# VectorE makes every low part of the weights, low parts of the input projection are re-read from DRAM, and the work is put in a new order

## The chip, the cores and the metric

The kernel runs on one core of a Trainium2 chip. The metric is the device time of one execution in microseconds; the median of three runs counts. Five engines work side by side: TensorE (PE in the rows; its weight loads are PEld), VectorE (DVE), ScalarE (ACT), GpSimd (POOL) and SyncE (SP), which here does nothing but issue DMAs. Each engine takes its instructions strictly in their order; an instruction that has to wait holds up all that stand behind it on its engine.

## The reference, cut to what matters

One layer of a decoder trunk over a prompt of 1040 tokens (16 learned ones ahead) and 32 sample tokens, all float32:

```python
def _layer(x, ...):
    xn = _rms(x, norm1_g)
    u = jnp.einsum('bld,de->ble', xn, w_in)              # input projection, 1024 -> 2816
    u_tm, u_lx, u_lg = jnp.split(u, [D_TM_PROJ, D_TM_PROJ + D_LRU], axis=-1)
    y_tm, ... = _rwkv7(u_tm, ...)                        # matrix recurrence over the tokens, 8 heads of 64
    y_lru, ... = _rglru(u_lx, u_lg, ...)                 # gated linear recurrence over the tokens
    x = x + jnp.einsum('ble,ed->bld', jnp.concatenate([y_tm, y_lru], axis=-1), w_out)
    xn = _rms(x, norm2_g)
    up = jnp.einsum('bld,df->blf', xn, ffn_w_up)         # 1024 -> 3072
    upc, ... = _causal_dwconv(up, ffn_conv, ffn_conv_w, ffn_conv_b)
    hid = jax.nn.gelu(upc) * jnp.einsum('bld,df->blf', xn, ffn_w_gate)
    x = x + jnp.einsum('blf,fd->bld', hid, ffn_w_down)
    return x, ...
```

Outputs are the normed activations and five kinds of state.

## The kernel before, in words

**Matmuls and low parts.** Each weight is split into a high part `wh` (rounded to the fast matmul format) and a low part `wl`, the rest; activations are split likewise. `load_w` (L529 to L540) brings 1024 x 128 weights in two halves of 256 KB: a DMA into `wraw` (L534), a ScalarE copy that rounds into `wh` (L537), and a subtraction that makes `wl` (L538), on VectorE for the first half and on GpSimd for the second. `wraw`, `wh` and `wl` have rings of four halves, that is two calls. `mm_tile` (L542) adds three products for each of eight slices of 128 rows, `wl` by the activation's high part (L546), `wh` by the same (L547), `wh` by its low part (L548), into one PSUM bank `mmb`; there are two such banks.

**The first stage** (everything up to the line with `issue_in_order`) is written as steps in the list `ORDER`. Tokens come in two pieces, of 560 and of 512. `x` norms and transposes a piece (`xt`, `xh`, `xl`, L517 to L524); `p`, `q` and `l` are its input projection, 22 calls of `load_w` for each piece, so that each weight of `w_in` is loaded, rounded and split twice; `proj` computes a tile in the piece's two column chunks `chk` (280 and 280, or 256 and 256) and a ScalarE copy empties each bank into `stage` (L755). `u` is a unit of the matrix recurrence (four heads, up to 256 tokens): a long run of VectorE work, small matmuls, and two round trips through DRAM (`zd` to `Dq`, `xd` to `WD`). `r` is the gated recurrence. `w` is the output projection for a quarter of the tokens (L1410 to L1423), `n` and `f` (`fac`, L1467 to L1476) an early part of the up and gate projections, and `e` the last quarter of `w_out` with the second norm (`xn`, `n2h`, `n2l`, L1547 to L1551).

**What sets the order.** `plan` takes the steps' instructions and what each must wait for, gives each instruction a duration from `cost`, and schedules them engine by engine, those with the longest way to the end first; what it finds is fixed as each engine's order. It holds GpSimd and VectorE apart where both read SBUF through operands. For a GpSimd subtraction that writes the fast matmul format, `cost` gives VectorE's duration.

**The second stage** (`up_gate`, `down`) is written out: up and gate projection of 128 columns at a time, the rest of the tokens, then the down projection (L1642 to L1645).

Of the kernel before, what the change touches and what calls it, by code (L numbers as in the profile page):

```python
# [12 lines left out]
F32 = mybir.dt.float32  # L13
F32R = mybir.dt.float32r
# [7 lines left out]
P = 128  # L22
# [28 lines left out]
class Piece:  # L51
    def __init__(self, idx, g0, gw):
        self.idx, self.g0, self.gw = idx, g0, gw
        self.chk = [(0, gw // 2), (gw // 2, gw // 2)]
# [23 lines left out]
ORDER = [('l', 0), ('p', 0, 0), ('u', 0, 0, 0), ('u', 0, 0, 1), ('q', 0, 0, 1), ('r', 0, 0), ('u', 0, 0, 2), ('p', 0, 1), ('r', 0, 1), ('q', 0, 2, 3), ('x', 1), ('r', 0, 2), ('l', 1), ('u', 0, 1, 0), ('q', 1, 0, 1), ('p', 1, 1), ('u', 0, 1, 1), ('r', 0, 3), ('u', 0, 1, 2), ('r', 1, 0), ('u', 1, 1, 0), ('p', 1, 0), ('q', 1, 2, 3), ('w', 0), ('n',), ('u', 1, 1, 1), ('f', 0, 0), ('f', 0, 1), ('u', 1, 0, 0), ('f', 1, 0), ('f', 2, 0), ('f', 1, 1), ('r', 1, 1), ('f', 3, 0), ('f', 2, 1), ('w', 1), ('f', 3, 1), ('f', 4, 0), ('f', 5, 0), ('u', 1, 0, 1), ('r', 1, 2), ('f', 4, 1), ('f', 5, 1), ('f', 6, 0), ('r', 1, 3), ('w', 2), ('f', 7, 0), ('e',), ('f', 6, 1), ('f', 7, 1)]  # L78
# [9 lines left out]
STREAM, FILL = 1.05, 10.8  # L88

TOGETHER = {}  # L90
TABLES = {"Exp": "e", "Sqrt": "s", "Gelu_apprx_tanh": "g"}
# [100 lines left out]
def cost(x):  # L192
# [7 lines left out]
    if e == "PE":  # L200
# [5 lines left out]
        side = 1  # L206
        if i[0].dtype == F32R:
            parts, cols, w = 1, n * STREAM + FILL, n
        elif getattr(x, "is_transpose", False):
            parts, cols, w = 1, 2 * n, 2 * n * (k == P)  # L210
        else:
            parts, cols, w = 2, 2 * n, 4 * n * (k >= 64)
            side = P // min(shape)
            cols += side * FILL * (side > 1)
# [4 lines left out]
    if e == "Activation":  # L219
        return (0.051 if psum else 0.093) + n / 1200 + 0.093 * s, None  # L220
    if e == "DVE" or o and o[0].dtype == F32R:
        fast = len(i) - s < 2 and not psum and "Memset" not in type(x).__name__
        return 0.069 + n / (1920 if fast else 960) + 0.061 * s, None
# [149 lines left out]
def hymba_kernel(ctx: ExitStack, tc: tile.TileContext, ins, outs, dbg=None):  # L373
# [156 lines left out]
    def load_w(src, c0):  # L530
        hs = []
        for k in (0, 4):
# [5 lines left out]
            (G if k else V).tensor_sub(l, raw, h.bitcast(F32))  # L538
# [20 lines left out]
    r = 0  # L559
# [190 lines left out]
    def proj(pc, xn, ti, func=AF.Copy):  # L750
        wh, wl = load_w(w_in, P * ti)
# [630 lines left out]
    def wout(pc, tmp, x1=None, stage=None):  # L1382
# [13 lines left out]
        for m in range(8):  # L1396
            wh, wl = load_w(w_out, P * m)
# [354 lines left out]
```

## Time and profile before

| | us |
|---|---|
| median of three runs (lowest to highest) | 1641.05 (1639.43 to 1644.85) |
| the profiled execution, its own time | 1638.3 |
| its span, first to last instruction | 1636.6 |
| TensorE busy in it | 1516.7 |
| VectorE busy | 1049.6 |
| ScalarE busy | 739.7 |
| GpSimd busy | 406.9 |

The span is read in stretches: the first piece's input projection up to about 230 us, a changeover to the second piece (230 to 300), the second piece's input projection (300 to 500), output projection and early up and gate projection (500 to 917), and the second stage from 917 to the end. For each stretch the table of windows gives what each engine was busy, the clock that TensorE was granted (1.00 is 2.4 GHz, 0.50 is 1.2 GHz; a stretch between shows a mixture of the two), and the load of the DMA engines. What TensorE was not busy in a stretch, and what its clock was below 1.00, is time that another order or other durations could give back.

### The profile page before, as it was taken

The page shows a single profiled execution, that of the slowest core. Times are in us where ns is not written, and L with a number is a line of the kernel's source. Part 1 is how long each engine was busy: PE and PEld are TensorE (multiplying, and loading weights), DVE is VectorE, ACT ScalarE, POOL GpSimd, SP SyncE. Part 2 cuts the span into 40 slices and gives each one's busy share as a digit, 9 for nine tenths or more (in the row PEclk, how much of TensorE's full clock was granted, in tenths as well). Part 3 has the DMA queues.
Part 4 walks back from the last instruction along what each step waited for, and adds up shares of the span by engine and source line. Part 5 has one row for each costly group of instructions (what it writes and reads, how often), then busy time and mean ns, then how long its engine had stood idle before and what let it go on. Part 6 is the DMA issues. An engine that isn't in the chain of part 4 may idle for free. (4 is left out here: it accounts for less than half of the span.)

```text
span 1636.6 us, 32363 instructions
## 1 busy us (share of the span) xinstructions
PE 1516.7 (93%) x12364; PEld 1428.5 (87%) x12364; DVE 1049.6 (64%) x2306; ACT 739.7 (45%) x1577; POOL 406.9 (25%) x580
## 2 busy tenths in 40 slices
PE   5999988999988978888897999999999999999997
PEld 5988876888877877777787899999999999999996
DVE  7376768877872999699568654554554455455446
ACT  4457377565653666567555433223223223222312
POOL 4232224332324433544344211011001001101101
PEclk9999989999999989999999999999999999999999
DMA  6544334444555445645577421121122112212102
GB/s 167 156 127 123 109 92 123 142 131 116 145 147 144 138 124 138 188 127 149 159 197 204 144 86 55 55 66 56 56 62 66 52 55 68 60 55 63 39 17 108
DMA packets 321791, 176.35 MB, mean 108 GB/s; under 512 B 70088, under 2 KB 309436, under 8 KB 321604
## 3 DMA queue, kind: packets, MB, share of 16 engines
q1 hardware_dynamic: 315796, 172.56, 37.0%
q10 hardware_dynamic: 5840, 1.73, 0.5%
q8 instruction: 97, 1.59, 0.4%
q14 instruction: 58, 0.48, 0.1%
HBM read 143.57 MB, written 30.85 MB: 107 GB/s over the span
## 5 line engine op out<-in xcount | busy, mean ns | idle before, releaser
L538 POOL TENSOR_TENSOR wl<-wraw,wh 128x512 fp32r<-128x512 f32 x172 | 230.0, 1338 | 343.2 <-ACT wh L537 330.1
L537 ACT ACTIVATE wh<-wraw 128x512 fp32r<-128x512 f32 x344 | 213.2, 627 | 166.5 <-PE mmb L548 112.2
L546 PE MATMUL mmb<-n2h,wl 128*128 128x400 f32 (+1 forms) x768 | 265.6, 346 | 3.8 <-DVE fac L1467 3.8
L548 PE MATMUL mmb<-n2l,wh 128*128 128x400 f32 (+1 forms) x768 | 265.9, 346 | 0.0
L547 PE MATMUL mmb<-n2h,wh 128*128 128x400 f32 (+1 forms) x768 | 265.3, 345 | 0.0
L538 DVE TENSOR_TENSOR wl<-wraw,wh 128x512 fp32r<-128x512 f32 x172 | 135.7, 789 | 168.4 <-ACT wh L537 166.1
L1645 DVE TENSOR_TENSOR x<-x,mmb 128x352 f32<-128x352 f32 (+3 forms) x288 | 149.5, 520 | 88.6 <-PE mmb L1644 82.9
L1642 PE MATMUL mmb<-hh,dl 128*128 128x352 f32 (+3 forms) x576 | 188.9, 328 | 1.7 <-DVE x L1645 0.4
L1643 PE MATMUL mmb<-hh,dh 128*128 128x352 f32 (+3 forms) x576 | 186.7, 324 | 0.0
L1644 PE MATMUL mmb<-hl,dh 128*128 128x352 f32 (+3 forms) x576 | 186.3, 323 | 0.0
L546 PE MATMUL mmb<-xh,wl 128*128 128x280 f32 (+1 forms) x704 | 156.9, 301 | 5.7 <-ACT stage L755 5.6
L547 PE MATMUL mmb<-xh,wh 128*128 128x280 f32 (+1 forms) x704 | 152.1, 294 | 0.0
L548 PE MATMUL mmb<-xl,wh 128*128 128x280 f32 (+1 forms) x704 | 151.0, 294 | 0.0
L546 PEld LDWEIGHTS mmb<-n2h,wl 128*128 128x128 f32 x768 | 145.2, 189 | 4.2 <-DVE fac L1467 4.0
L547 PEld LDWEIGHTS mmb<-n2h,wh 128*128 128x128 f32 x768 | 145.3, 189 | 0.0
L548 PEld LDWEIGHTS mmb<-n2l,wh 128*128 128x128 f32 x768 | 144.9, 189 | 0.0
L546 PE MATMUL mmb<-yxh,wl 128*128 128x258 f32 (+1 forms) x384 | 111.8, 310 | 24.8 <-DVE fac L1467 9.5
L1635 ACT ACTIVATE dh<-draw 128x256 fp32r<-128x256 f32 x96 | 39.8, 416 | 190.3 <-PE mmb L1644 186.8
L546 PEld LDWEIGHTS mmb<-xh,wl 128*128 128x128 f32 x704 | 113.1, 191 | 13.3 <-ACT stage L755 8.8
L548 PEld LDWEIGHTS mmb<-xl,wh 128*128 128x128 f32 x704 | 111.9, 191 | 2.8 <-issue 1.6
L547 PEld LDWEIGHTS mmb<-xh,wh 128*128 128x128 f32 x704 | 112.6, 192 | 1.7
L1587 POOL COPY us<-up 128x32 f32<-128x32 f32 x24 | 5.1, 211 | 438.1 <-ACT up L1586 438.1
(447 smaller groups left out, 3232.3 us busy)
## 6 DMA issues: line engine op xcount, KB each, us to landing
wraw<-in_ffn_w_up_dram SPq DMA_DIRECT2D x96, 256.0 KB
wraw<-in_ffn_w_gate_dram SPq DMA_DIRECT2D x96, 256.0 KB
wraw<-in_w_in_dram SPq DMA_DIRECT2D x88, 256.0 KB
wraw<-in_w_out_dram SPq DMA_DIRECT2D x64, 256.0 KB
draw<-in_ffn_w_down_dram SPq DMA_DIRECT2D x96, 128.0 KB
ul<-uscr SPq DMA_DIRECT2D x24, 257.0 KB
uscr<-stage SPq DMA_DIRECT2D x20, 280.0 KB
uscr<-stage SPq DMA_DIRECT2D x20, 256.0 KB
```

What stands on the lines that cost most here:

```text
L537: S.activation(h, raw, AF.Copy)
L538: (G if k else V).tensor_sub(l, raw, h.bitcast(F32))
L546: PE.matmul(bk[:, :n], wl[k], mh[:, k, c0:c0 + n], start=(k == 0), stop=False)
L547: PE.matmul(bk[:, :n], wh[k], mh[:, k, c0:c0 + n], start=False, stop=False)
L548: PE.matmul(bk[:, :n], wh[k], ml[:, k, c0:c0 + n], start=False, stop=(k == nk - 1))
L1587: G.tensor_copy(us[:, :, 2:6], up[:, 1026 - AH:].rearrange("p (b t) -> p b t", b=NS))
L1635: S.activation(wh, raw, AF.Copy)
L1642: PE.matmul(bk[:, :n], wl[:, j, :], hh[:, o:o + n], start=(j == 0), stop=False)
L1643: PE.matmul(bk[:, :n], wh[:, j, :], hh[:, o:o + n], start=False, stop=False)
L1644: PE.matmul(bk[:, :n], wh[:, j, :], hl[:, o:o + n], start=False, stop=(j == len(hids) - 1))
L1645: V.tensor_add(x1[:, m, 2 + o:2 + o + n], x1[:, m, 2 + o:2 + o + n], bk[:, :n])
```

## The change

`load_w` makes both halves' low parts on VectorE. In the first piece's input projection (`keep`) each low half is also stored to a DRAM tile of its own (`lows`); in the second piece's, where the same weights come again, the low half is read from there by a DMA into `wl`, and no subtraction is made; the high part is still loaded as `wraw` and rounded by ScalarE. A piece of at most 512 tokens is one chunk of 512 columns. `cost` and its constants get other numbers: for a matmul of the fast format, for short ScalarE and VectorE instructions, for scans, and for GpSimd, whose subtractions no longer have VectorE's price. `ORDER` is another list.

```diff
 class Piece:
-        self.chk = [(0, gw // 2), (gw // 2, gw // 2)]
+        self.chk = [(0, gw)] if gw <= 512 else [(0, gw // 2), (gw // 2, gw // 2)]
...
-ORDER = [('l', 0), ('p', 0, 0), ('u', 0, 0, 0), ('u', 0, 0, 1), ('q', 0, 0, 1), ('r', 0, 0), ('u', 0, 0, 2), ('p', 0, 1), ('r', 0, 1), ('q', 0, 2, 3), ('x', 1), ('r', 0, 2), ('l', 1), ('u', 0, 1, 0), ('q', 1, 0, 1), ('p', 1, 1), ('u', 0, 1, 1), ('r', 0, 3), ('u', 0, 1, 2), ('r', 1, 0), ('u', 1, 1, 0), ('p', 1, 0), ('q', 1, 2, 3), ('w', 0), ('n',), ('u', 1, 1, 1), ('f', 0, 0), ('f', 0, 1), ('u', 1, 0, 0), ('f', 1, 0), ('f', 2, 0), ('f', 1, 1), ('r', 1, 1), ('f', 3, 0), ('f', 2, 1), ('w', 1), ('f', 3, 1), ('f', 4, 0), ('f', 5, 0), ('u', 1, 0, 1), ('r', 1, 2), ('f', 4, 1), ('f', 5, 1), ('f', 6, 0), ('r', 1, 3), ('w', 2), ('f', 7, 0), ('e',), ('f', 6, 1), ('f', 7, 1)]
+ORDER = [('l', 0), ('p', 0, 0), ('u', 0, 0, 0), ('u', 0, 0, 1), ('q', 0, 0, 1), ('p', 0, 1), ('r', 0, 0), ('u', 0, 0, 2), ('q', 0, 2, 3), ('x', 1), ('r', 0, 1), ('q', 1, 2, 3), ('r', 0, 2), ('l', 1), ('u', 0, 1, 0), ('u', 0, 1, 1), ('u', 0, 1, 2), ('q', 1, 0, 1), ('r', 0, 3), ('p', 1, 1), ('r', 1, 0), ('u', 1, 1, 0), ('u', 1, 1, 1), ('p', 1, 0), ('w', 0), ('n',), ('f', 0, 0), ('u', 1, 0, 0), ('f', 0, 1), ('f', 1, 0), ('f', 2, 0), ('w', 1), ('f', 1, 1), ('u', 1, 0, 1), ('r', 1, 1), ('f', 3, 0), ('f', 2, 1), ('f', 3, 1), ('f', 4, 0), ('f', 4, 1), ('f', 5, 0), ('f', 5, 1), ('f', 6, 0), ('r', 1, 2), ('r', 1, 3), ('w', 2), ('f', 7, 0), ('e',), ('f', 7, 1), ('f', 6, 1)]
...
-STREAM, FILL = 1.05, 10.8
+STREAM, FILL = 1.0, 26
+LOWS = 'I'
...
-        return (0.051 if psum else 0.093) + n / 1200 + 0.093 * s, None
-    if e == "DVE" or o and o[0].dtype == F32R:
+        return (0.051 if psum else 0.093) + n / 1200 + 0.093 * s + 0.05 * (n <= 128), None
+    if getattr(x, "is_tensor_tensor_scan", False):
+        return 0.15 + n / 480, None
+    if e == "DVE":
         fast = len(i) - s < 2 and not psum and "Memset" not in type(x).__name__
-        return 0.069 + n / (1920 if fast else 960) + 0.061 * s, None
+        return 0.069 + n / (1920 if fast else 960) + 0.061 * s + 0.05 * (n <= 128 and psum), None
     if "TensorTensor" in type(x).__name__:
         return (0.3 + 0.165 * n if n <= 8 else 0.154 + n / 480), None
...
-    def load_w(src, c0):
+    lows = {}
+
+    def load_w(src, c0, keep=False):
...
             S.activation(h, raw, AF.Copy)
-            (G if k else V).tensor_sub(l, raw, h.bitcast(F32))
+            name = f"{src.tensor.name}_{c0}_{k}"
+            if name in lows:
+                SY.dma_start(l.bitcast(F32).rearrange("p a b -> p (a b)"), lows[name])
+            else:
+                V.tensor_sub(l, raw, h.bitcast(F32))
+                if keep:
+                    lows[name] = dram.tile([P, 4 * P], F32, name="low" + name)
+                    SY.dma_start(lows[name], l.bitcast(F32).rearrange("p a b -> p (a b)"))
...
     def proj(pc, xn, ti, func=AF.Copy):
-        wh, wl = load_w(w_in, P * ti)
+        wh, wl = load_w(w_in, P * ti, 'I' in LOWS and pc.idx == 0)
```

Three places where the instructions now stand otherwise; lines of the changed kernel are up to 13 higher.

TensorE within the second piece's input projection, before (two matmuls of 256 columns, one for each chunk, with the same weights):

```order
L546 MATMUL mmb<-xh,wl 128x256 x2
L547 MATMUL mmb<-xh,wh 128x256 x2
L548 MATMUL mmb<-xl,wh 128x256 x2
L546 MATMUL mmb<-xh,wl 128x256 x2
L547 MATMUL mmb<-xh,wh 128x256 x2
```

and now, within the same projection:

```order
L559 MATMUL mmb<-xh,wl 128x512
L561 MATMUL mmb<-xl,wh 128x512
L560 MATMUL mmb<-xh,wh 128x512
L559 MATMUL mmb<-xh,wl 128x512
L561 MATMUL mmb<-xl,wh 128x512
```

Each pair became one matmul of 512 columns; at some places two tiles with different weights alternate, each in one of the two banks.

VectorE in the changeover to the second piece, from the sixth `xt` scaling to the fifth of the eight `xl` subtractions, before (the rows between are of the gated recurrence, `kp`, `v`, and of a unit, `carry`, `SV`, `mean`):

```order
L517 SCALAR_TENSOR_TENSOR xt<-xt,rsy,g1r 128x512
L1173 SCALAR_TENSOR_TENSOR carry<-kb,PC,svp 64x64
L1296 SCALAR_TENSOR_TENSOR kp<-Pt,kp 128x560
L1173 SCALAR_TENSOR_TENSOR carry<-kb,PC,svp 64x64
L1138 COPY SV<-carry 64x2x64 x2
...
L1282 SCALAR_TENSOR_TENSOR v<-uls,prmT,v 128x32
L1276 SCALAR_TENSOR_TENSOR v<-ul,prmT,v 128x528
L1299 MEMSET kp 128x1
L1282 SCALAR_TENSOR_TENSOR v<-uls,prmT,v 128x32
L1301 TENSOR_TENSOR kp<-kp,ta 128x560
L524 TENSOR_TENSOR xl<-bb,xh 128x4x128
```

and now, from the fourth `xl` to the sixth:

```order
L527 TENSOR_TENSOR xl<-bb,xh 128x4x128
L1186 SCALAR_TENSOR_TENSOR SV<-kb,PC,svp 64x64
L1088 TENSOR_TENSOR Qs<-lb,m_346 128x256
L516 TENSOR_SCALAR ms<-ssum 128x1
L1295 SCALAR_TENSOR_TENSOR v<-uls,prmT,v 128x32
L527 TENSOR_TENSOR xl<-bb,xh 128x4x128
L520 SCALAR_TENSOR_TENSOR xt<-xt,rsy,g1r 128x512 x2
L527 TENSOR_TENSOR xl<-bb,xh 128x4x128
```

Fewer instructions of the recurrences stand between the steps of the preparation: 45 instructions from the first `xl` to the last before, 32 now.

SyncE within the second piece's input projection, before (`wraw` are weights, `zd` and `Dq` a unit's first round trip, `uscr` what `proj` writes):

```order
L534 DMA wraw<-in_w_in_dram 128x4x128
L955 DMA zd_463<-ZB 32x8x32 x4
L961 DMA Dq<-zd_463 32x16x16 x2
L534 DMA wraw<-in_w_in_dram 128x4x128
L961 DMA Dq<-zd_463 32x16x16 x2
L765 DMA uscr<-stage 128x512
```

and now (`wl<-low...` are the stored low halves):

```order
L546 DMA wl<-lowin_w_in_dram_4_2213 128x512
L540 DMA wraw<-in_w_in_dram 128x4x128
L778 DMA uscr<-stage 128x512
L546 DMA wl<-lowin_w_in_dram_0_2275 128x512
L540 DMA wraw<-in_w_in_dram 128x4x128
L861 DMA dg<-loscr 64x2x256 x2
L1277 DMA ul<-uscr 128x560
```

The 44 reads of low halves stand among the weights' and the units' DMAs; each waits until TensorE has done with the half that its buffer held.

## Rows read from the trace of the kernel before

**Rows 1.** The page: busy time by engine, and granted clock in 40 slices.
```profile
PE 1516.7 (93%) x12364; PEld 1428.5 (87%) x12364; DVE 1049.6 (64%) x2306; ACT 739.7 (45%) x1577; POOL 406.9 (25%) x580
...
PEclk9999989999999989999999999999999999999999
```

**Rows 2.** Windows: stretch, length, busy us (instructions) by engine, granted clock, DMA share, GB/s.
```profile
25.00:230.00 205.00, 197.18 (x1916) 179.25 (x1914) 129.57 (x365) 103.81 (x244) 49.86 (x76) 1.00 0.46 129
230.00:300.00 70.00, 57.58 (x595) 48.38 (x590) 63.45 (x166) 55.07 (x130) 27.62 (x42) 0.88 0.38 112
300.00:500.00 200.00, 188.93 (x1996) 169.65 (x1997) 151.85 (x347) 110.75 (x248) 58.51 (x71) 0.98 0.50 137
...
545.00:660.00 115.00, 96.82 (x813) 88.53 (x811) 105.17 (x216) 74.30 (x144) 45.13 (x41) 0.94 0.52 140
660.00:715.00 55.00, 48.25 (x810) 42.98 (x809) 41.82 (x106) 34.85 (x80) 27.57 (x33) 0.97 0.56 161
715.00:775.00 60.00, 50.55 (x460) 44.19 (x459) 57.30 (x118) 42.17 (x73) 24.08 (x23) 0.96 0.50 142
775.00:850.00 75.00, 67.89 (x772) 62.79 (x773) 43.41 (x99) 38.53 (x86) 32.42 (x36) 0.93 0.59 166
850.00:917.00 67.00, 53.15 (x381) 50.36 (x381) 54.63 (x122) 36.16 (x92) 27.09 (x25) 0.93 0.73 212
917.00:1600.00 683.00, 681.77 (x3904) 677.19 (x3903) 340.10 (x625) 196.40 (x363) 75.29 (x140) 1.00 0.21 59
```

**Rows 3.** Waits of TensorE: releaser, us in total, times, longest.
```profile
PE mmb L546 <- DVE fac L1467: 13.3, 8, 3.8
...
PE mmb L546 <- DVE Pt L927: 6.0, 1, 6.0
...
PE mmb L546 <- DVE fac L1472: 3.2, 3, 1.9
...
PE mmb L1410 <- POOL wl L538: 2.1, 1, 2.1
```

**Rows 4.** The line that makes low parts: duration min/median/max in ns.
```profile
L538 DVE TENSOR_TENSOR wl<-wraw,wh x172: 673/692/1937, 20.2 to 1551.8; 128x512 fp32r<-128x512 f32 x172
L538 POOL TENSOR_TENSOR wl<-wraw,wh x172: 1253/1292/2123, 20.3 to 1554.1; 128x512 fp32r<-128x512 f32 x172
```

**Rows 5.** Timeline 600 to 608 us, all engines: start, us, engine, line, xcount [idle before].
```profile
600.47 1.23 SPq L848 DMA_DIRECT2D dg<-loscr  x2
...
600.79 2.49 POOL L538 TENSOR_TENSOR wl<-wraw,wh 128x512 fp32r<-128x512 f32 x2 [2.55 <-ACT wh L537]
600.84 1.26 DVE L921 COPY PC<-Pt 128x8 f32<-128x8 f32 x1
...
602.01 1.95 DVE L773 SCALAR_TENSOR_TENSOR r<-ul,prmT,r 128x256 f32<-128x256 f32 x2
...
604.08 0.47 DVE L1472 SCALAR_TENSOR_TENSOR fac<-mmb,frmT,fac 128x256 f32<-128x256 f32 x1
604.40 0.63 ACT L850 ACTIVATE twh<-dg 128x512 fp32r<-128x512 f32 x1 [2.13 <-DMA dg<-loscr]
...
607.11 0.55 PE L546 MATMUL mmb<-yxh,wl 128*128 128x256 f32 x1 [5.97 <-DVE Pt L927]
```

**Rows 6.** Timeline, TensorE alone, second piece's input projection (pairs of 256 columns).
```profile
321.13 0.40 PE L548 MATMUL mmb<-xl,wh 128*128 128x256 f32 x2
...
322.57 0.40 PE L548 MATMUL mmb<-xl,wh 128*128 128x256 f32 x2
```

**Rows 7.** Timeline, TensorE alone, down projection at the end (512 columns).
```profile
1594.46 0.39 PE L1643 MATMUL mmb<-hh,dh 128*128 128x512 f32 x1
...
1597.92 0.40 PE L1643 MATMUL mmb<-hh,dh 128*128 128x512 f32 x1
```

**Rows 8.** Waits of SyncE's queue: releaser, us in total, times, longest.
```profile
SPq L534 <- DVE wl L538: 296.3, 89, 9.0
...
SPq L534 <- POOL wl L538: 167.0, 92, 5.6
```

More of the change, by code (lines that the diff above doesn't have):

```diff
@@ L213, in cost @@
             side = P // min(shape)
-            cols += side * FILL * (side > 1)
+            cols += side * 10.8 * (side > 1)
         return parts * (max(cols, 2 * m) / 2400 / side + 0.0025), (parts, cols / 2400 / side, 2 * m / 2400 / side, first,
@@ L1396, in wout @@
         for m in range(8):
-            wh, wl = load_w(w_out, P * m)
+            wh, wl = load_w(w_out, P * m, 'O' in LOWS and pc.idx == 0)
             dst = tmp("x1t", m) if x1 is None else None
```

## Prediction

> **What bounds the kernel now.** I read the page first: TensorE is busy 93% of the span, VectorE 64%, GpSimd 25%, and TensorE's granted clock dips in two of 40 slices, both in the first half [rows 1]. The windows by stretch come second, and there the reader is to see two kernels in one [rows 2]. From 917 us on TensorE is idle 1.2 of 683 us at full clock: bound by matmuls, and only fewer or shorter matmuls would shorten it. Before that it is idle in every stretch, and its clock drops. What was lost in a stretch is its length less TensorE's busy time, plus the part of the clock that was not granted. First piece, 25 to 230: 7.8 us. Changeover, 230 to 300: 12.4 idle and 70 x 0.12 = 8.4 in clock, 20.8. Second piece, 300 to 500: 11.1 and 4.0, 15.1. From 545 to 917 the five windows add up to 55.3 idle (18.2, 6.8, 9.4, 7.1, 13.8) and, with 0.94, 0.97, 0.96, 0.93 and 0.93, to 20.9 in clock (6.9, 1.7, 2.4, 5.2, 4.7): 76. So some 120 us are there to be had, nearly two thirds of them after 545.
>
> Who ends the waits is the third view. `fac` and `Pt` are VectorE's, 13.3, 6.0 and 3.2 us; a low part from GpSimd ends a wait of 2.1 us itself [rows 3]. VectorE is busy 105 of 115 us in 545 to 660 and 57 of 60 in 715 to 775, against 152 of 200 in 300 to 500 [rows 2]. The late part of the first stage is thus bound by VectorE where TensorE waits most.
>
> The timeline shows how GpSimd makes that worse [rows 5]. At 600.79 GpSimd starts two low parts, 2.49 us. In that time VectorE runs a copy of 128 x 8 that lasts 1.26, and two `r` instructions of 256 columns that take 1.95, where an instruction of the same kind and width takes 0.47 just after. About 1.2 and 1.0 us went to waiting beside GpSimd, and TensorE, behind VectorE's queue, stands for 5.97 us.
>
> **Matmul width.** Six pairs of 256-column matmuls start from 321.13 to 322.57, 0.240 us a pair [rows 6]; fifteen matmuls of 512 columns from 1594.46 to 1597.92, 0.231 each [rows 7]. The second piece's projection has 22 tiles x 8 slices x 3 products = 528 pairs: 528 x 0.0093 = 4.9 us less. Ends: 3 and 6. TensorE has nothing else to do there, so this lies on the path.
> The Trainium skill (TensorE: Matmul & The Clock Gate, Back-to-back issue gap) gives an isolated matmul N/2.4 + 2.5 ns at full clock, 109 and 216 ns here; by it the pairs would give back only 528 x 2.5 ns = 1.3 us. The rows show 120 and 231 ns, so a larger fixed part than the page has; the rows decide.
>
> **The low parts.** VectorE takes 0.69 us for one, GpSimd 1.29 (medians) [rows 4]. Of the 172 that GpSimd made, 22 belong to the second piece's projection and go, as do 22 of VectorE's there; 150 move, so VectorE gets 150 - 22 = 128 more, 128 x 0.69 = 88 us. Against that stands what 172 GpSimd instructions took from it. Lower bound: nothing at all, when VectorE runs what GpSimd does not disturb. Upper bound: 1.29 each. In the dense place of rows 5 two of them took about 2.2 us, 1.1 each; but VectorE idles a third of the span, and there they take nothing. I take 0.6 in the first stage, which makes a move nearly neutral, 0.69 against 0.6. By stretch:
>
> First piece: 22 moved, 22 x (0.69 - 0.6) = 2 us on an engine that is busy 130 of 205; TensorE covers it. Its ends are 22 x 0.69 = 15 more and 22 x 0.6 = 13 less, both under the 75 us that VectorE idles. 44 stores of 256 KB, 11.5 MB in 205 us, add 56 GB/s to 129, against 212 that the stretch 850 to 917 sustains. I cost both at nothing (-3 to +4 on TensorE's 7.8 us of idling). Without that cover the 15 us would be paid.
>
> Second stage: 48 of 683 us' VectorE instructions are added, 48 x 0.69 = 33 on 340 busy. TensorE has 1.2 us of idling there, so no gain; a low part in front of the additions that empty `mmb` could cost half a microsecond in each of the 12 rounds. Nothing, 0 to +6.
>
> **Changeover, 230 to 300.** VectorE is busy 63.5 of 70 us [rows 2]; TensorE has only a unit's short matmuls until the second piece is prepared. By the order of instructions 45 stand on VectorE from the first `xl` to the last before and 32 now. 13 x (63.45/166 = 0.38) = 5 us sooner, and some of the five or six low parts on either engine that fell into the stretch are gone: 3 us. 8 us of the 20.8. Ends: 0 and 16.
>
> **Second piece against the late part.** On VectorE, between the last `xl` and the first row of `w_out`, units (with their token shifts) have 435 instructions now and 345 before, the gated recurrence 54 and 37, low parts 4 and 24. After it units have 324 and 403, low parts 160 and 80. Late part: 80 x 0.69 = +55, 79 x 0.49 (105.17/216) = -39, 80 x 0.6 = -48: 32 less of 302 busy, a tenth. With the lock at nothing it would be +16, with 1.1 a -72. In 545 to 660 and 715 to 775, 175 us, TensorE loses 27.6 idle and 9.3 in clock; at the level of the second piece, 15.1 in 200 us, it would lose 13. The difference is 24 and I take half, because a tenth less work does not take VectorE from 93% to 76%: -12, ends 0 and -24. Second piece: 20 low parts less (-14), their neighbours on GpSimd gone (-13), 90 unit instructions at 0.44 (+39) and 17 of the recurrence at 0.75 or less (+13): 152 becomes about 177 in a stretch that also gets the units' matmuls. I cost it +3 (0 to +8).
>
> **Sum** against the profiled execution, 1638.3 with 1636.6 of span: -4.9 - 8 - 12 + 3 = -21.9, 1616.4. The median of the runs is 1641.05, 0.2% above the profiled one; the sum is not moved for that.
>
> **Rivals.**
> The lock is worth all of it. If every GpSimd low part takes its whole 1.29 us from VectorE, the dense windows reach the second piece's level (-24), the end of the first stage (850 to 917, 18.5 lost) gets half back (-9), the changeover 13: 4.9 + 24 + 9 + 13 - 3 = 48 less, 1590. For it: rows 5. Against: VectorE's median low part is 0.69, though each call of `load_w` has one on GpSimd at about the same time [rows 4]. The Trainium skill (SBUF — State Buffer, SBUF: two separate sides) says just this: VectorE with two SBUF inputs and GpSimd share one port pair as an exclusive lock, and the loser is blocked for the whole instruction. Rows 5 agree at their place; how often it is so, they don't show.
>
> Only the name changes. VectorE's own low parts take what the lock took, and the units that moved ahead crowd the second piece: the late part keeps its 76 us, the changeover gives 3, the width 4.9: 1630. For it: over the whole kernel VectorE gets 88 us and is freed of 172 x 0.6 = 103, which is nearly nothing on 1049.6.
>
> SyncE's queue blocks, and the kernel is slower. 44 reads of low halves now wait for TensorE to free a half of the ring, and SyncE holds all that stands behind: the next weights, the units' `Dq` and `WD`. A call of `load_w` now takes 24 x 0.231 = 5.5 us; where two tiles alternate, a half is freed only 5.5 us before its successor is needed. A transfer of 128 KB issued until 601.70 has its reader start at 604.40, 2.7 us [rows 5]; with twice the size some 3.5. That leaves 2 us, and SyncE waits 3.3 us on average for VectorE's low part before it issues a weight, up to 9.0 [rows 8]. If each of the 22 calls comes 2 us late, 44 us are lost: 1660. It decides from 1 us a call, which eats the 22 gained. Against: in the second piece a weight's buffer no longer waits for a subtraction on VectorE or GpSimd, 296 and 167 us of SyncE's waits, and the DMA engines are half idle (0.50).
>
> **How the numbers follow.** Forecast 0.50, lock worth all of it 0.14, only the name 0.18, SyncE 0.18. A measurement here tells about 0.3% from no change, 5 us. Faster by more: nearly all of the forecast (0.47), the first rival (0.14), half of the second (0.09), 0.01 of the third: 0.71. Within: 0.03 + 0.07 + 0.02 = 0.12. Slower: 0.17. The terms' ends all together give 1592 and 1653 (-46 and +15, the second stage's +6 and the first piece's +4 among them); that they all fall on one side is unlikely, and at half the distance the forecast's own range is 1604 to 1635; reaching into the first and third rival it is 1590 to 1650.
>
> **What would show it.** Width: starts of 512-column matmuls 0.231 apart in the second piece. Low parts: VectorE's mean for one falls to its median, and instructions that lasted over 1.2 us for short rows are gone. Changeover: TensorE's idling and clock in the stretch before the first 512-column matmul lose less than 20.8 us. Late part: TensorE's waits on `fac` and `Pt` shrink and the second stage starts near 895 instead of 917. The third rival would be seen as waits of TensorE for `wl` from DRAM, and of SyncE at L546 for TensorE. I am wrong if VectorE is busier than before in the late part, or if the second stage, which I leave at its length, gets a wait in each round.

## Result, and the profile after

The changed kernel takes 1613.65 us (median of runs from 1610.17 to 1616.21); the kernel before, run beside it, 1640.24 (1638.67 to 1644.85). The ratio is 0.983, 95% interval 0.980 to 0.986: 1.7% faster. The forecast was 1616.4. The profiled execution took 1612.6 with a span of 1610.8, 25.8 less than the 1636.6 of before.

The page of the changed kernel: busy time by engine, the granted clock in 40 slices, and the line that makes low parts (instructions | busy us, mean ns | idle before it).

```profile
PE 1511.2 (94%) x11836; PEld 1389.6 (86%) x11836; DVE 1055.0 (65%) x2434; ACT 737.2 (46%) x1552; POOL 176.6 (11%) x408
...
PEclk9999989999998899999999999999999999999999
...
L548 DVE TENSOR_TENSOR wl<-wraw,wh 128x512 fp32r<-128x512 f32 x300 | 209.7, 703 | 230.5 <-ACT wh L543 215.4
```

Beside [rows 1]: GpSimd is relieved of 230 us, VectorE has 128 instructions more and is busy only 5.4 us longer. TensorE's busy time fell by 5.5, its idling from 119.9 to 99.6. The gain is idling: 20.3 of 25.8.

Where it went is read from windows whose ends are events and not fixed times: the first piece's projection, the changeover, the second piece's projection, the late part of the first stage, the second stage. First the kernel before, then the changed one (stretch, length, busy us and instructions of PE, PEld, DVE, ACT, POOL, granted clock, DMA share, GB/s).

```profile
23.90:221.80 197.90, 191.61 (x1717) 175.40 (x1715) 125.18 (x353) 96.34 (x221) 46.60 (x68) 1.00 0.47 131
221.80:255.80 34.00, 24.04 (x404) 17.60 (x402) 28.60 (x68) 32.07 (x74) 11.44 (x23) 0.80 0.34 105
255.80:462.10 206.30, 198.08 (x2063) 177.83 (x2062) 170.03 (x399) 122.40 (x279) 69.07 (x90) 0.99 0.46 130
462.10:912.60 450.50, 381.75 (x4054) 345.78 (x4052) 344.19 (x766) 267.09 (x574) 184.33 (x186) 0.94 0.56 156
912.60:1636.60 724.00, 714.12 (x4108) 706.63 (x4108) 365.27 (x679) 209.14 (x401) 80.18 (x149) 1.00 0.21 63
```

```profile
23.70:219.60 195.90, 188.31 (x1630) 174.23 (x1629) 128.37 (x356) 90.20 (x207) 18.11 (x45) 0.98 0.64 191
219.60:247.60 28.00, 21.93 (x336) 16.66 (x335) 20.56 (x51) 23.56 (x61) 6.74 (x15) 0.70 0.59 159
247.60:476.40 228.80, 220.47 (x2036) 161.49 (x2034) 186.57 (x484) 154.14 (x330) 49.84 (x88) 0.99 0.58 166
476.40:887.20 410.80, 358.42 (x3705) 324.02 (x3703) 330.08 (x780) 246.62 (x528) 68.53 (x94) 0.94 0.61 171
887.20:1610.80 723.60, 714.92 (x4108) 707.96 (x4108) 374.34 (x720) 210.06 (x397) 20.60 (x103) 0.99 0.21 63
```

The lengths differ by -2.0, -6.0, +22.5, -39.7 and -0.4. TensorE's busy time fell by 3.3 and 2.1 in the first two, which have fewer of its instructions now. In the second piece 22.4 us of TensorE's work were added and 23.3 left the late part: those are the units that the list moved ahead, and no loss or gain. What counts is idling: it is 8.2 and 8.3 in the second piece, and 68.8 and 52.4 in the late part. The other 3.9 are the changeover's (10.0 to 6.1). In the second stage VectorE has 9 us more to do, and its length did not change.

Waits of TensorE in the changed kernel (releaser, us in total, times, longest):

```profile
PE mmb L559 <- DVE fac L1480: 7.4, 5, 3.3
...
PE mmb L559 <- DVE fac L1485: 3.2, 4, 1.4
...
PE mmb L559 <- DVE wl L548: 1.2, 1, 1.2
```

Of [rows 3], the first row on `fac` fell from 13.3 to 7.4, the second stayed at 3.2, and the waits on `Pt` (6.0) and on GpSimd's `wl` (2.1) are gone.

### The profile page after: what moved, and what is told of

It is laid out like the page before. It is cut to its first block, busy times and chain, and to the rows that moved or that the text cites. A ratio compares the mean times of both kernels' runs of the same rounds, so it can differ in the third digit from the quotient of the medians.

```text
span 1610.8 us, 31369 instructions
## 1 busy us (share of the span) xinstructions
PE 1511.2 (94%) x11836; PEld 1389.6 (86%) x11836; DVE 1055.0 (65%) x2434; ACT 737.2 (46%) x1552; POOL 176.6 (11%) x408
## 4 chain that ended last, share of the span: by engine, by line
PE 67%; DVE 12%; DMA 9%; ACT 6%; issue 4%; SPq 2%; POOL 0%; ACTq 0%; DVEq 0%; POOLq 0%
PE mmb L559 13%; PE mmb L560 13%; PE mmb L561 13%; PE mmb L1655 6%; PE mmb L1656 6%; PE mmb L1657 6%; DVE wl L548 2%; DMA wraw<-in_w_out_dram 1%; ACT wh L543 1%; DMA stage<-in_x_prompt_dram 1%; DVE yc L1252 1%; DMA wraw<-in_w_in_dram 1%; PE mmb L1423 1%; PE bb L957 1%; PE mmb L1428 1%
## 5 line engine op out<-in xcount | busy, mean ns | idle before, releaser
L548 DVE TENSOR_TENSOR wl<-wraw,wh 128x512 fp32r<-128x512 f32 x300 | 209.7, 703 | 230.5 <-ACT wh L543 215.4
L1656 PE MATMUL mmb<-hh,dh 128*128 128x352 f32 (+3 forms) x576 | 186.6, 324 | 0.0
L559 PE MATMUL mmb<-xh,wl 128*128 128x280 f32 (+1 forms) x528 | 152.1, 347 | 7.6 <-ACT stage L768 7.6
L560 PE MATMUL mmb<-xh,wh 128*128 128x280 f32 (+1 forms) x528 | 148.7, 341 | 0.0
L561 PE MATMUL mmb<-xl,wh 128*128 128x280 f32 (+1 forms) x528 | 146.7, 338 | 0.0
L559 PE MATMUL mmb<-yxh,wl 128*128 128x256 f32 (+1 forms) x384 | 108.4, 301 | 11.8 <-DVE fac L1480 4.0
L1655 PEld LDWEIGHTS mmb<-hh,dl 128*128 128x128 f32 x576 | 108.2, 188 | 4.2 <-DVE x L1658 3.6
L559 PEld LDWEIGHTS mmb<-xh,wl 128*128 128x128 f32 x528 | 91.9, 194 | 21.0 <-ACT stage L768 11.2
L1657 PEld LDWEIGHTS mmb<-hl,dh 128*128 128x128 f32 x576 | 108.3, 188 | 0.7
L1656 PEld LDWEIGHTS mmb<-hh,dh 128*128 128x128 f32 x576 | 108.3, 188 | 0.4
L560 PE MATMUL mmb<-yxh,wh 128*128 128x256 f32 (+1 forms) x384 | 104.8, 292 | 0.0
```

Of the source, the lines that this page charges most:

```text
L548: V.tensor_sub(l, raw, h.bitcast(F32))
L559: PE.matmul(bk[:, :n], wl[k], mh[:, k, c0:c0 + n], start=(k == 0), stop=False)
L560: PE.matmul(bk[:, :n], wh[k], mh[:, k, c0:c0 + n], start=False, stop=False)
L561: PE.matmul(bk[:, :n], wh[k], ml[:, k, c0:c0 + n], start=False, stop=(k == nk - 1))
L1655: PE.matmul(bk[:, :n], wl[:, j, :], hh[:, o:o + n], start=(j == 0), stop=False)
L1656: PE.matmul(bk[:, :n], wh[:, j, :], hh[:, o:o + n], start=False, stop=False)
```

## Theories, and experiments

Four theories stand in the expectations. A, the forecast's: moving low parts to VectorE is about neutral, and the gain comes from what was taken out of the second piece and from the units that moved there. B: GpSimd's subtractions were the cost, by the lock (VectorE stands while GpSimd's subtraction runs, as in [rows 5]) or by coming late. C: the new list is all of it. D: each new plan is a draw, and the difference is chance.

"Span" below is that of the profiled execution. All ratios are against the kernel before, run beside it. The kernel before took 1640.24 to 1645.45 us from one set of runs to another, so sets are compared by their ratios and not by their times.

### One part of the change on the kernel before

**Low parts all on VectorE**, with the old list.

```diff
-            (G if k else V).tensor_sub(l, raw, h.bitcast(F32))
+            V.tensor_sub(l, raw, h.bitcast(F32))
```

> The kernel before with one edit: VectorE makes both halves' low parts (172 more subtractions on VectorE, none on GpSimd); list, prices and chunks as before, nothing kept in DRAM. Theory A (the gain comes from the second piece's freed VectorE time and from units moved there): VectorE gets 172 x 0.69 = 119 us and is freed of about 103, so the time stays within 5 us of 1640. Theory B (GpSimd's lock and lateness were the cost): 15 us or more faster, 1625 or less. Theory C (the list of steps is all): no change.

Measured: 1626.47 us, ratio 0.990 (0.988 to 0.993). The late part, first to last line of the two stretches before the second stage (columns as above):

```profile
257.70:462.80 205.10, 198.24 (x2128) 178.77 (x2126) 169.65 (x422) 123.69 (x281) 35.16 (x67) 0.99 0.47 130
462.80:903.50 440.70, 382.54 (x3988) 344.23 (x3987) 354.65 (x847) 266.64 (x573) 78.89 (x105) 0.93 0.58 160
```

VectorE is busy 10.5 us longer in the late part, and the late part is 9.8 us shorter. One word, without list or store, is worth 1%. That is more than A's nearly neutral move, and VectorE's busy time has the wrong sign to explain it. The word also takes the planner's wrong price for GpSimd's subtractions out of play, and the order is planned anew; what the price alone is worth is the third experiment here.

**One chunk of 512 columns.**

```diff
-        self.chk = [(0, gw // 2), (gw // 2, gw // 2)]
+        self.chk = [(0, gw)] if gw <= 512 else [(0, gw // 2), (gw // 2, gw // 2)]
```

> The kernel before with one edit: the second piece is one chunk of 512 columns. All theories: 528 pairs x 0.0093 us = 4.9 us faster, 1635; faster than that only if the free second bank saves waits on `stage`; the 512-column matmuls start 0.231 us apart.

Measured: 1642.70 us, ratio 0.999 (0.998 to 1.001). No gain. In its second piece:

```profile
256.90:467.90 211.00, 198.19 (x1463) 147.37 (x1460) 164.07 (x391) 120.94 (x254) 66.54 (x88) 0.95 0.43 121
```

TensorE's busy time is that of before (198.08), the granted clock 0.95 instead of 0.99, the idling 12.8 instead of 8.2. What the pairs gave back by themselves is hidden under that and under a new plan; it did not arrive.

**The planner's price for GpSimd's subtractions.**

```diff
-    if e == "DVE" or o and o[0].dtype == F32R:
+    if e == "DVE":
```

> The kernel before with one edit: the planner's price of GpSimd subtractions is GpSimd's (1.22 us) and not VectorE's (0.60); the work is the same. Theory A: some of the waits behind VectorE in 545 to 660 and 715 to 775 go, 3 to 8 us faster. Theory B: no gain, since the lock itself stays. Theory C: no change or slower, since the list was chosen under the old price.

Measured: 1636.28 us, ratio 0.996 (0.995 to 0.997). A planner that knows that GpSimd is slow loses 0.4% less, as A expected.

**The new list alone** (the `ORDER` of the changed kernel).

```diff
-ORDER = [('l', 0), ('p', 0, 0), ('u', 0, 0, 0), ('u', 0, 0, 1), ('q', 0, 0, 1), ('r', 0, 0), ('u', 0, 0, 2), ('p', 0, 1), ('r', 0, 1), ...
+ORDER = [('l', 0), ('p', 0, 0), ('u', 0, 0, 0), ('u', 0, 0, 1), ('q', 0, 0, 1), ('p', 0, 1), ('r', 0, 0), ('u', 0, 0, 2), ('q', 0, 2, 3), ...
```

> The kernel before with one edit: the new list of steps, all else as before. Theory A: units move into the second piece's stretch, but it still has its 44 subtractions on VectorE and GpSimd; about half of what was won in the late part, 5 to 10 us faster, 1630 to 1635. Theory B: no change. Theory C: 15 us or more faster, 1625 or less.

Measured: 1653.68 us, ratio 1.007 (1.005 to 1.010): slower. C falls. The second piece and the late part:

```profile
243.70:509.40 265.70, 241.94 (x2575) 212.07 (x2572) 218.36 (x512) 159.38 (x353) 82.31 (x111) 0.92 0.39 108
509.40:927.00 417.60, 363.43 (x3696) 328.79 (x3694) 308.73 (x685) 245.29 (x522) 176.52 (x174) 0.93 0.59 165
```

The late part becomes 32.9 us shorter (39.7 in the changed kernel), but the second piece 59.4 longer: it has 24 us of idling (8 before) and a clock of 0.92. The units were moved into a stretch that has no room for them.

### One part taken out of the changed kernel

**The old list.** The edit is the same two lines of `ORDER`, the other way round.

> The changed kernel with one edit: the list of steps of the kernel before. Theory A: the second piece's stretch has VectorE time to spare and the late part gets its units back, and the changeover its recurrences: 10 to 18 us slower, 1624 to 1632. Theory B: less than 5 us slower. Theory C: the whole gain goes, 1635 or more.

Measured: 1635.56 us, ratio 0.996 (0.993 to 0.998).

```profile
253.90:456.30 202.40, 195.66 (x1495) 146.44 (x1496) 147.54 (x391) 127.91 (x268) 38.86 (x71) 0.98 0.63 185
456.30:908.80 452.50, 382.34 (x4126) 344.45 (x4124) 361.40 (x862) 270.24 (x580) 75.18 (x105) 0.94 0.57 158
```

Here the second piece has room (VectorE busy 148 of 202 us) and nobody uses it; the late part is as long as before. So the list costs 0.7% on the kernel before and gives 1.2% on the changed one (0.996 against 0.983). This is the interplay that A names.

**Low parts of the second piece made again**, not read from DRAM.

```diff
-LOWS = 'I'
+LOWS = ''
```

> The changed kernel with one edit: no low part is kept in DRAM, VectorE makes those of the second piece too (44 more subtractions, 30 us; 22.5 MB less of DMA). Theory A: the second piece's stretch, where VectorE is busy 187 of 229 us, gets 30 us more and lengthens by 10 to 20: 1624 to 1634. Theory B: within 5 us of 1614, since no GpSimd work comes back. Theory C: no change.

Measured: 1631.36 us, ratio 0.994 (0.991 to 0.996).

```profile
241.70:493.20 251.50, 232.98 (x2048) 172.42 (x2046) 210.05 (x524) 156.67 (x334) 51.27 (x89) 0.94 0.40 111
493.20:908.30 415.10, 360.24 (x3705) 325.42 (x3703) 329.14 (x783) 247.45 (x529) 70.17 (x96) 0.94 0.60 169
```

The second piece takes 22.7 us longer, idles 18.5 instead of 8.3, and the clock is 0.94. The 44 subtractions that the store spares are what makes the room.

**Every other low part back on GpSimd**, planned as such.

```diff
-                V.tensor_sub(l, raw, h.bitcast(F32))
+                (G if k else V).tensor_sub(l, raw, h.bitcast(F32))
```

> The changed kernel with one edit: the second half's low parts are made by GpSimd again where they are made at all (150 subtractions); the planner prices them as GpSimd's. Theory A: the move is nearly neutral, 3 to 8 us slower than 1614. Theory B: most of the gain goes, 1630 or more. Theory C: no change.

Measured: 1635.80 us, ratio 0.996 (0.993 to 0.998). The plan differs from the changed kernel's here, so that the price and the draw are mixed; the next run separates them.

**The same, with the order of the changed kernel.** The planner treats GpSimd's subtractions as VectorE's, so that all engines keep their planned order, and GpSimd takes its 150 out of VectorE's row.

```diff
+def planned_on(x):
+    e = engine_of(x)
+    return "DVE" if e == "Pool" and aps(x.outs) and aps(x.outs)[0].tensor.name.startswith("wl") else e
...
-    order = plan(insts, dependencies(insts, before, after), t0)[1]
+    begin = plan(insts, dependencies(insts, before, after), t0)[2]
+    order = defaultdict(list)
+    for i in sorted(range(len(insts)), key=lambda i: (begin[i], i)):
+        order[engine_of(insts[i])].append(i)
...
-                V.tensor_sub(l, raw, h.bitcast(F32))
+                (G if k else V).tensor_sub(l, raw, h.bitcast(F32))
```

> The changed kernel, with the order of the first stage frozen as the changed kernel's planner made it (the same rows on every engine), and one edit: the 150 second halves that are made at all are made by GpSimd, each at the time at which VectorE made it. Theory A (a move is nearly neutral): VectorE gives up 150 x 0.69 and loses 150 x 0.56, 0 to 8 us slower than 1614. Theory B (lock and lateness count): VectorE's busy time hardly changes, but a low part comes 1.3 us or more after its rounding instead of 0.7, in front of TensorE: 15 us slower or more. Theory D (most of the 22 us of the run with GpSimd's second halves was another order found by the planner): within 5 us of 1614, with the second piece's stretch at 229 us instead of 243.

Measured: 1631.23 us, ratio 0.992 (0.990 to 0.995), and the changed kernel's 0.983 (0.980 to 0.986) lies outside: 0.9% or some 15 us by the ratios. Span 1628.3, 17.5 more. The late part:

```profile
480.20:904.60 424.40, 360.73 (x3705) 328.02 (x3703) 316.34 (x698) 247.53 (x528) 173.68 (x176) 0.94 0.59 165
```

VectorE has 13.7 us less to do than in the changed kernel, and the stretch is 13.6 us longer; TensorE idles 63.7 instead of 52.4. No wait of TensorE ends on GpSimd's `wl`, so the low parts were not late. TensorE's waits add up to 15.7 us more than in the changed kernel: those that end on VectorE, over all its tiles, to 62.4 against 54.7, those on ScalarE to 4.5 more, and the other 3.5 are almost all on DMAs.

Which rows of VectorE became longer in the late part shows where the lock falls. Two groups of the changed kernel, and then of this run (instructions | busy us, mean ns | idle before):

```profile
L548 DVE TENSOR_TENSOR wl<-wraw,wh 128x512 fp32r<-128x512 f32 x163 | 114.2, 708 | 32.4 <-ACT wh L543 30.8 <-ACT stage L1443 0.2
...
L1564 DVE TENSOR_TENSOR n2l<-xn,n2h 128x256 fp32r<-128x256 f32 x24 | 10.3, 434 | 0.1
```

```profile
L558 DVE TENSOR_TENSOR wl<-wraw,wh 128x512 fp32r<-128x512 f32 x81 | 66.0, 815 | 33.1 <-ACT wh L553 30.4 <-DMA wraw<-in_ffn_w_up_dram 2.1 <-issue 0.2
...
L1574 DVE TENSOR_TENSOR n2l<-xn,n2h 128x256 fp32r<-128x256 f32 x24 | 14.7, 614 | 1.3 <-ACT n2h L1573 1.0
```

VectorE gives up 82 low parts, and those that it keeps take 815 ns instead of 708. Of its other rows `n2l`, an input of matmuls, gains the most time, 4.4 us: 614 ns instead of 434.

### The lock by itself

**A subtraction on GpSimd whose result nobody reads**, beside VectorE's own (150 of them). VectorE's own work stays what it was.

```diff
                 V.tensor_sub(l, raw, h.bitcast(F32))
+                if k:
+                    G.tensor_sub(raw, raw, h.bitcast(F32))
```

> The changed kernel with one addition: after VectorE has made a second half's low part, GpSimd makes the same difference once more, over `wraw`, which nothing reads (150 GpSimd subtractions of 128x512 beside the work; the next load into that buffer waits for them). VectorE's own work is unchanged, so the time over 1614 is what GpSimd takes from it. Theory A: 0.6 us each, three quarters of them in the first stage, mostly where VectorE has room: 8 to 15 us slower. Theory B: 1.1 us each, 25 us slower or more.

Measured: 1666.65 us, ratio 1.015 (1.012 to 1.017). Slower than the kernel before, by work that nobody needs on an engine that even so is busy only 23% of the span. The plan is not the changed kernel's here; the next run has its order.

**The same with the changed kernel's order**, the unread subtractions left out of the plan and put in behind it.

```diff
+def aside(x):
+    return engine_of(x) == "Pool" and bool(aps(x.outs)) and aps(x.outs)[0].tensor.name.startswith("wraw")
...
+    kept = [x for x in insts if not aside(x)]
+    begin = dict(zip((x.name for x in kept), plan(kept, dependencies(kept, before, after), t0)[2]))
+    for a, b in zip(insts, insts[1:]):
+        if aside(b):
+            begin[b.name] = begin[a.name] + 0.6
```

> The changed kernel with its first stage's order frozen, and GpSimd's 150 extra subtractions that nothing reads beside it. VectorE's work and order are unchanged, so this is the lock alone, without the planner's luck. Theory A: VectorE is busy 80 us longer, 0.56 for each, nearly half of it in the second stage where TensorE doesn't wait; 15 to 30 us slower than 1614. Theory B: 1.1 us each where VectorE is dense, 50 us slower or more, as in the run with a new order. Theory D: the second piece's stretch, where none of them runs, is back at 229 us, and the time is about 16 us under the 1667 of the run with a new order.

Measured: 1683.57 us, ratio 1.025 (1.022 to 1.028); span 1679.0, 68.2 more than the changed kernel's. The five stretches:

```profile
22.80:230.70 207.90, 192.84 (x1630) 178.40 (x1629) 137.45 (x351) 90.35 (x207) 48.91 (x67) 0.95 0.59 180
230.70:258.40 27.70, 20.54 (x338) 15.26 (x336) 21.34 (x56) 23.74 (x61) 6.60 (x15) 0.75 0.61 162
258.40:487.40 229.00, 219.45 (x2036) 160.51 (x2034) 186.47 (x484) 154.26 (x330) 49.42 (x88) 1.00 0.58 166
487.40:945.90 458.50, 367.69 (x3704) 328.60 (x3702) 380.54 (x780) 248.35 (x528) 184.14 (x174) 0.93 0.54 153
945.90:1679.00 733.10, 718.01 (x4108) 707.04 (x4108) 402.18 (x720) 206.41 (x397) 84.17 (x152) 0.99 0.21 62
```

With the same instructions on VectorE, its busy time over the five rises from 1039.9 (the sum over the changed kernel's five) to 1128.0: 88.1 us, 0.59 for each GpSimd instruction. The second piece, which has none of them, is where it was (186.5 and 186.6 us of VectorE, 229.0 and 228.8 in length). In the late part VectorE gets 50.5 us, and the stretch becomes 47.7 us longer; the first piece grows by 12.0, the second stage by 9.5. (The second stage has just under a third of the 150, and not nearly half as the expectation says.) D's guess has the wrong sign: this run is slower than the one with a new order, not faster. Two things are mixed in here. The unread result also holds `wraw` longer, and SyncE waits for it 207.8 us in 94 times:

```profile
SPq L551 <- POOL wraw L561: 207.8, 94, 6.2
```

And on GpSimd the unread subtraction waits for VectorE's low part and holds up what stands behind it. TensorE's waits that end on `wl` stay at 1.2 us in all. Of 53.7 us that its waits gain, 37.6 end on VectorE, 9.4 on ScalarE and 5.8 on DMAs. So most of TensorE's added waiting goes through VectorE, but not all of the 68.2 need be the lock.

Which instructions of VectorE are hit can be read line by line. The changed kernel, and then this run, VectorE's groups of the second stage by line and shape (instructions | busy us, mean ns | idle before):

```profile
L1658 DVE TENSOR_TENSOR x<-x,mmb 128x352 f32<-128x352 f32 (+3 forms) x288 | 149.7, 520 | 84.6 <-PE mmb L1657 78.2
L1609 DVE SCALAR_TENSOR_TENSOR acc<-up,frmT,acc 128x768 f32<-128x768 f32 x48 | 48.8, 1016 | 15.2 <-ACT acc L1607 15.2
...
L1617 DVE TENSOR_TENSOR acc<-acc,mmb 128x400 f32<-128x400 f32 x48 | 27.4, 572 | 44.5 <-ACT acc L1613 24.0 <-PE mmb L561 20.5
L1619 DVE TENSOR_TENSOR hl<-acc,hh 128x400 fp32r<-128x400 f32 x48 | 27.4, 572 | 13.9 <-ACT hh L1618 13.9
```

```profile
L1671 DVE TENSOR_TENSOR x<-x,mmb 128x352 f32<-128x352 f32 (+3 forms) x288 | 148.6, 520 | 84.9 <-PE mmb L1670 79.3
L1622 DVE SCALAR_TENSOR_TENSOR acc<-up,frmT,acc 128x768 f32<-128x768 f32 x48 | 69.3, 1444 | 15.2 <-ACT acc L1620 15.2
...
L1632 DVE TENSOR_TENSOR hl<-acc,hh 128x400 fp32r<-128x400 f32 x48 | 37.1, 774 | 13.9 <-ACT hh L1631 13.9
...
L1630 DVE TENSOR_TENSOR acc<-acc,mmb 128x400 f32<-128x400 f32 x48 | 27.4, 571 | 30.4 <-ACT acc L1626 24.0 <-PE mmb L574 6.4
```

Two lines with the same operation and width part ways: `hl` goes from 572 to 774 ns, `acc<-acc,mmb` stays at 571. The first reads two tiles of SBUF, the second one tile and a bank that TensorE filled. The timeline of the run with the unread subtractions shows one collision, GpSimd's and VectorE's rows:

```profile
1002.46 1.28 POOL L561 TENSOR_TENSOR wraw<-wraw,wh 128x512 f32<-128x512 f32 x1 [4.74 <-DVE wl L559]
```

```profile
1002.29 0.52 DVE L1671 TENSOR_TENSOR x<-x,mmb 128x352 f32<-128x352 f32 x1
1002.72 1.44 DVE L1632 TENSOR_TENSOR hl<-acc,hh 128x400 fp32r<-128x400 f32 x1
```

The addition at 1002.29 reads a bank, overlaps GpSimd from 1002.46 on, and takes its usual 0.52. The subtraction behind it takes 1.44 instead of 0.57, since GpSimd is at work until 1003.74. In the late part more than half of the 50.5 us, 26.8, falls on VectorE's own low parts (163 low parts take 873 ns on average instead of 708):

```profile
L559 DVE TENSOR_TENSOR wl<-wraw,wh 128x512 fp32r<-128x512 f32 x163 | 141.0, 873 | 25.7 <-ACT wh L554 24.4 <-issue 0.2
```

What TensorE waited for in the same run:

```profile
PE mmb L572 <- DVE fac L1493: 15.6, 8, 4.7
...
PE mmb L1668 <- DVE x L1671: 6.6, 12, 0.6
```

The first of these rows stood at 7.4; the second, one wait in each of the twelve rounds of the second stage, is a single wait of 0.3 in the changed kernel. A plan that knows of the unread subtractions is 1.0% or some 16 us better than this one (ratios 1.015 and 1.025), so a frozen order is not a better order; it only keeps the price apart from the plan.

### The draw, and an attempt to go on

**The old constants for matmuls**, in the changed kernel.

```diff
-STREAM, FILL = 1.0, 26
+STREAM, FILL = 1.05, 10.8
```

> The changed kernel with one edit: the planner's old price of a fast matmul (1.05 n + 10.8 cycles instead of n + 26), which is 3 ns less for 256 columns and 4 ns more for 512. The work is the same and the prices hardly differ. Theories A, B: within 3 us of 1614. Theory D (a planned order is a draw, any small difference gives another one): up to 15 us off, mostly to the slower side, since the list was chosen under the new price.

Measured: 1620.28 us, ratio 0.986 (0.983 to 0.990), an interval that overlaps the changed kernel's. (The old price of 256 columns is 1 ns less, not 3: 279.6 cycles and 282.) By the ratios this plan of the same work costs 0.3%, some 5 us, which is not clear of noise; in the profiled executions the second piece (+6.3) and the late part (+3.7) are longer. The two pairs above that have the same work under two plans differ by 0.3% (GpSimd's second halves) and 1.0% (unread subtractions). Draws of this size don't make 1.7%, but they can hide or feign a part of it. The new prices for short instructions and scans were not tried alone, and one chunk was not taken out of the changed kernel.

**Low parts of the output projection kept too.**

```diff
-LOWS = 'I'
+LOWS = 'IO'
```

The changed kernel has this second letter prepared: `w_out`'s low parts are stored in its first pass and read in the three others.

> The changed kernel with one edit: the low parts of the output projection are kept in DRAM by its first quarter too and read by the other three (48 subtractions fewer in the late part, 33 us of VectorE; 16 stores and 48 loads of 256 KB more). Theory A: VectorE, busy 330 of 411 us there, loses a tenth of its work: 5 to 10 us faster than 1614. Theory B: the same, 5 us faster. Theory D: any sign, -5 to +15, since the list was chosen without it.

Measured: 1624.55 us, ratio 0.989 (0.986 to 0.991): faster than before, slower than the changed kernel.

```profile
475.00:899.50 424.50, 364.78 (x3705) 331.35 (x3703) 295.51 (x726) 246.18 (x524) 63.33 (x94) 0.92 0.71 204
```

VectorE has 34.6 us less in the late part, which yet becomes 13.7 us longer, with 7.3 us more idling, a clock of 0.92 and 204 instead of 171 GB/s. Waits of TensorE on `stage<-in_x_prompt_dram` go from 3.1 to 6.2, and six waits, 2.7 us in all, end on a low half of `w_out` read back. Whether it is the transfers or the new plan isn't settled by this run. That fewer us of VectorE do not by themselves shorten the late part is seen once more. No run was faster than the changed kernel.

## Why the prediction was right, and where it was not

The total came within 3 us of the median (1616.4 and 1613.65), and the stretches where the time was sought are those where it was found. That it fits so well is in part luck. One of the reasons was wrong, and terms were mis-sized in opposite directions: for the second piece and the late part together the forecast has -4.9 + 3 - 12 = -13.9, and they took 17.2 less (+22.5 and -39.7), but not for those reasons.

**Low parts on VectorE: the step that failed.** The lock's price was about right: 0.6 us was taken for a GpSimd low part, 0.59 was measured beside the unread subtractions, and about 0.5 where GpSimd made its 150 (VectorE gave up 150 x 0.70 = 105 us, and its busy time fell by 28.9). The step "which makes a move nearly neutral, 0.69 against 0.6" is what failed. It subtracts one amount of VectorE's busy time from another, as if an us of either cost TensorE the same. The runs with the frozen order show that they don't. In the late part the unread subtractions put 50.5 us on VectorE, and the stretch became 47.7 longer: 0.94 for each. From that run to the one in which GpSimd makes its 150 low parts instead, VectorE loses 64.2 us (380.54 to 316.34), and the stretch only 34.1: 0.53. Over the whole kernel, with the order kept: 68.2 us lost through 150 unread subtractions, 50.7 given back by 150 low parts less, and so 17.5 gained by moving them. The forecast took nothing for this; by its busy times it would have been a loss of 13 (150 x 0.09). The low parts alone, on the old list, go the same way: 1% faster with VectorE busier, where the planner's price alone is worth 0.4%.

Why the one us costs more than the other is argued here and not shown. A low part is made ahead of need, and TensorE hardly ever waits for one (1.2 us); a lock lengthens whatever VectorE just runs, and `n2l` and `hl`, which feed matmuls, are among the rows that became longer. But much of the lock falls on low parts too, and the later loads have a share. Nor does VectorE simply have time to spare where it makes low parts: of the 230.5 us for which it idles before line 548, 172.1 lie in the second stage and 32.4 in the late part.

The Trainium skill (SBUF — State Buffer, SBUF: two separate sides) has the lock between GpSimd and a VectorE instruction with two SBUF inputs. The rows agree on who is hit, `hl` and not `acc<-acc,mmb`; an instruction that reads one bank keeps its 571 ns.

**The first rival, the lock worth all of it,** was nearer to the mechanism, but its price was too high: it reckoned 1.29 us for each instruction, the runs show 0.59 and less, and its time, 1590, is 24 us under the measured one.

**Late part: -12 forecast.** Idling fell from 68.8 to 52.4, with the clock at 0.94 in both: 16.4, between the term and its end of 24. The forecast's own reason, 32 us less on VectorE, was less than half so large (344.2 to 330.1). With the order kept and GpSimd making its second halves, the idling is 63.7. So 11.3 of the 16.4 belong to the step above, for which the forecast took nothing, and 5.1 are left for the units that moved ahead, for which it took 12. That the term came near is luck. The signs that the forecast named did appear: TensorE's waits on `fac` and `Pt` shrank, VectorE's mean for a low part fell from 789 to 703 ns (median 691), and the second stage starts at 887.2. The sign that I named for being wrong, VectorE busier in the late part, appeared in the run with VectorE's low parts alone, and time fell all the same: it was the wrong sign to look for.

**Second piece: +3 forecast.** Idling 8.2 and 8.3, clock 0.99 in both: nothing. Without the store it is 18.5. The forecast had the mechanism, 20 low parts less make room for 90 unit instructions; it took a little too much.

**Changeover and first piece: -8 and 0 forecast.** Together 231.9 became 223.9, which is -8.0: -6.0 and -2.0. The stores cost little: the first piece idles 7.6 instead of 6.3, at a clock of 0.98. The gain is the list: with the old list and all else changed the two take 230.3 (23.60 to 253.90), with the new list alone 220.4 (23.30 to 243.70). The part of the 8 that was put down to low parts (3 us) is not seen: with all of them on VectorE and the old list the second piece starts at 257.7, and at 255.8 before. Of the idling 3.9 went; the clock fell to 0.70 and took some back.

**Matmul width: -4.9 forecast, mis-sized.** The changed kernel's longest run of nothing but 512-column matmuls, TensorE alone (start, us):

```profile
465.22 0.62 PE L561 MATMUL mmb<-xl,wh 128*128 128x512 f32 x2
...
468.43 0.63 PE L559 MATMUL mmb<-xh,wl 128*128 128x512 f32 x2
...
471.69 0.40 PE L560 MATMUL mmb<-xh,wh 128*128 128x512 f32 x1
```

From 465.22 on 28 matmuls start before the one at 471.69: 0.231 apart on average, as in [rows 7]. So the price of an undisturbed matmul was right. But such runs are rare. From 337.30 to 343.43 there are 27 of them, 0.236 apart, and in shorter runs 0.238 and more. Over all 438 places where one of them starts right behind another the median is 0.234, and 528 x (0.240 - 0.234) is 3 us, the term's lower end. Alone on the kernel before, even that did not arrive (ratio 0.998 to 1.001). The term assumed that TensorE has nothing else to do there; it has, the units and the recurrence stand in between, and a saving in a stretch is worth only what the plan does with it. In the changed kernel TensorE's busy time over the second piece and the late part together fell by 0.9.

**Second stage: 0 forecast.** 724.0 and 723.6. The run with unread subtractions shows the wait per round that was feared, 12 waits of up to 0.6: it comes with GpSimd's work, not with a low part in front of an addition, for it is absent where VectorE makes the same low parts alone.

**SyncE's queue** showed the first half of its rival and not the second. The queue waits for TensorE where it is about to read a low half back; the line has no waiter. SyncE's waits, and then the line itself in the changed kernel:

```profile
SPq L540 <- DVE wl L548: 428.0, 165, 6.2
...
SPq L546 <- PE mmb L559: 59.3, 21, 11.8
```

```profile
L546 SPq DMA_DIRECT2D wl<-lowin_w_in_dram x44: 319/376/867, 207.0 to 461.4; - x44
...
who waited for it (us, times):
```

A queue that stands for up to 11.8 us did no harm that the profile shows: no wait of TensorE ends on a low half from DRAM, and its waits on DMAs of any kind are 11.7 us in all (13.3 before). So the rival's 2 us of slack were an underestimate.

**Only the name changes** (1630) is near what the kernel takes without the store (1631.4) or with the old list (1635.6). With both it fails, and in its reason too: the late part did not keep its loss (idling 68.8 to 52.4).

## What to carry to other kernels

Busy time on an engine is no price. Here an us of low parts on VectorE cost the late part 0.53 and the second stage nothing, while an us that GpSimd's unread work put on VectorE came with 0.94. To get the price, keep the order and add the cost alone, and look for what else the added work holds up.

An order of work and the load on an engine have to be changed together. The same list was worth -0.7% with the second piece full and +1.2% with it freed; either change alone would have been thrown away or thought small.

With a planner in between, each edit brings a new plan, and in three pairs of plans the draw was worth 0.3% to 1.0%. A part of that size can be told from it only with the order kept.

## What the runs showed of the hardware

A GpSimd subtraction of 128 x 512 (1.28 us at 1002.46) takes 0.59 us from VectorE on average, and in the second stage from instructions with two SBUF operands: 128 x 768 goes from 1016 to 1444 ns, 128 x 400 from 572 to 774, while 128 x 400 and 128 x 352 that read a bank of TensorE stay at 571 and 520. A second operand is not always needed: the copy of 128 x 8 that lasts 1.26 us in [rows 5] reads one tile. I had thought of the lock as a tax on VectorE as a whole.

The clock goes with idling in these runs and adds a second loss: the second piece idles 8 us at a granted clock of 0.99 (1.00 is 2.4 GHz), 13 at 0.95 (512 columns alone) and 24 at 0.92 (new list alone).
